# Four contiguous 256 KB transfers per token pair instead of two of 512 KB over every second row

## Chip, cores, metric

The kernel runs on one core of a Trainium2 chip. The metric is device time in microseconds (us). Before the change it took 1339.5 us (median of 3 runs, 1335.49 to 1341.65).

## The reference

```python
B, S, D, H = 64, 1024, 1024, 16          # Dh = D // H = 64
route_logits = x @ route_w               # x: [B, S, D] float32, route_w: [D, H]
best_head = np.argmax(route_logits, -1)
for h in range(H):                       # experts: [H, Dh, Dh]
    out[:, :, h, :] = (x_heads[:, :, h, :] @ experts[h]) * (best_head == h)[:, :, None]
```

x and out are 268 MB each; both have to cross between DRAM and SBUF once.

## The kernel before

The 65,536 tokens are taken 256 at a time, as a "pair" of tiles: each of the 128 partitions holds two consecutive tokens, 8 KB. A pair is loaded, transposed on TensorE, multiplied with experts and router, masked, and stored. Loads run seven pairs ahead; there are ten input and six output buffers. SP issues all of the loads and stores. An issue is the instruction that starts a transfer; the transfer has landed when all sixteen DMA engines have raised its semaphore. In the profile PE and PEld are TensorE's matmuls and weight loads, DVE is VectorE, ACT ScalarE, POOL GpSimd, SP SyncE; a q after the name is the engine's own instruction queue.

```python
WAYS = 2
XIN_BUFS, OUT_BUFS, AHEAD = 10, 6, 7     # (three lines of the kernel)
xg = x.rearrange("b s d -> (b s) d").rearrange("(g p t) d -> g p t d", p=P, t=2)
og = out.rearrange("b s d -> (b s) d").rearrange("(g p t) d -> g p t d", p=P, t=2)

def load(g):
    xin = xin_pool.tile([P, 2, D], FP32, name="xin", tag="xin")
    for r in range(WAYS):
        nc.sync.dma_start(out=xin[r::WAYS], in_=xg[g, r::WAYS])     # L106 in the profile
    return xin
# ... cut: constants, transposes (L115), split pass (L136), whole blocks (L150), ...
# ... finish(): VectorE (L173) and GpSimd (L181) write the masked products into ot
for j in range(-2 * AHEAD, NT + 2, 2):
    if j + 2 * AHEAD < NT:
        xins[j + 2 * AHEAD] = load(j // 2 + AHEAD)
    # ... cut: compute of the pair before
                if i == pair[1]:
                    for r in range(WAYS):
                        nc.sync.dma_start(out=og[i // 2, r::WAYS], in_=ot[r::WAYS])   # L223
```

The kernel names no semaphores; the framework makes them. The operands of SP's instructions in the trace show that its transfers use eight semaphores in turn, and that each issue first waits until the transfer that used its semaphore before has landed. So at most eight transfers are in flight.

## Time and profile before

| | before |
|---|---|
| time | 1339.5 us |
| TensorE busy; undisturbed pair | 96%; 4.926 us (256 x 4.926 = 1261) |
| SP's transfer queue, share of 16 engines | 98.6% |
| 8 KB data packets / 4-byte semaphore packets | 65,536 / 16,384 |
| data packet: median and floor | 309 ns |
| "held-up" time: what data packets last beyond that floor, sum of (duration - 309 ns) / 16 | 45 us per engine |
| issue to landing of a 512 KB transfer, median | 10.2 us |

The first lines are from the page of the kernel before: span, busy time of the compute engines, and the rate that the DMA engines moved in 40 equal slices of the span.

```profile
span 1338.1 us, 66342 instructions
...
PE 1290.3 (96%) x27648; PEld 1208.3 (90%) x27648; DVE 933.7 (70%) x4098; ACT 923.2 (69%) x1537; POOL 721.9 (54%) x1031
...
GB/s 340 421 421 416 413 407 409 407 407 406 412 398 377 418 417 399 395 412 414 398 393 404 410 416 418 402 408 397 410 407 410 412 407 417 416 405 416 417 409 327
```

The queue table of the kernel before gives packets, MB and the share of 16 engines' span. q1 holds SP's transfers; q8 brings instructions. The Trainium skill, "Runtime: NRT & Kernel Launch", section "Instruction fetch mechanics", says that each engine's instruction memory is refilled in blocks of 16 KiB, 256 instructions, through a DMA queue of its sequencer. This trace agrees: q8's packets have 16 KB, and TensorE's 55,296 instructions make 216 such blocks. I read q8 as TensorE's instruction fetch.

```profile
q1 hardware_dynamic: 81920, 536.94, 98.6%
q8 instruction: 218, 3.57, 1.0%
```

The chain that ended last (kernel before) is made of landings of stores, each followed by the issue that had waited for it:

```profile
DMA 96%; PE 1%; SPq 0%; DVE 0%; issue 0%; POOL 0%; ACT 0%; ACTq 0%; POOLq 0%; DVEq 0%
```

SP's own waits, kernel before (total us, times, longest): SP mostly waits for landings.

```profile
SPq L223 <- DMA out_dram<-ot: 373.2, 469, 1.7
SPq L106 <- DMA xin<-in_x_dram: 335.6, 496, 2.0
```

Issues of the kernel before, with KB each and median us from issue to landing:

```profile
xin<-in_x_dram SPq DMA_DIRECT2D x512, 512.0 KB, 10.2
out_dram<-ot SPq DMA_DIRECT2D x512, 512.0 KB, 10.2
```

SP's timeline in the middle of the kernel before (start us, length us, count). Two issues in a line of 1.7 us are each about 0.5 us long with a pause between them.

```profile
601.42 1.74 SPq L223 DMA_DIRECT2D out_dram<-ot  x2
603.92 1.68 SPq L106 DMA_DIRECT2D xin<-in_x_dram  x2
606.49 1.77 SPq L223 DMA_DIRECT2D out_dram<-ot  x2
609.03 1.65 SPq L106 DMA_DIRECT2D xin<-in_x_dram  x2
```

Waits of the compute engines, kernel before: a little time goes on output buffers whose stores are late.

```profile
DVE ot L173 <- DMA out_dram<-ot: 83.8, 104, 1.8
...
POOL ot L181 <- DMA out_dram<-ot: 76.3, 40, 3.0
```

### The profile page before, as it was taken

The page shows a single profiled execution, that of the slowest core. Times are in us where ns is not written, and L with a number is a line of the kernel's source. Part 1 is how long each engine was busy: PE and PEld are TensorE (multiplying, and loading weights), DVE is VectorE, ACT ScalarE, POOL GpSimd, SP SyncE. Part 2 cuts the span into 40 slices and gives each one's busy share as a digit, 9 for nine tenths or more (in the row PEclk, how much of TensorE's full clock was granted, in tenths as well). Part 3 has the DMA queues.
Part 4 walks back from the last instruction along what each step waited for, and adds up shares of the span by engine and source line. Part 5 has one row for each costly group of instructions (what it writes and reads, how often), then busy time and mean ns, then how long its engine had stood idle before and what let it go on. Part 6 is the DMA issues. An engine that isn't in the chain of part 4 may idle for free.

```text
span 1338.1 us, 66342 instructions
## 1 busy us (share of the span) xinstructions
PE 1290.3 (96%) x27648; PEld 1208.3 (90%) x27648; DVE 933.7 (70%) x4098; ACT 923.2 (69%) x1537; POOL 721.9 (54%) x1031
## 2 busy tenths in 40 slices
PE   7999999999999999999999999999999999999995
PEld 7888998999998999999998999889998999999995
DVE  4666766677776777777777677667777777767775
ACT  5666766767766777777676776667766767767673
POOL 3455555555555555555555555555555555555554
PEclk9999999999999999999999999999999999999998
DMA  8999999999999999999999999999999999999997
GB/s 340 421 421 416 413 407 409 407 407 406 412 398 377 418 417 399 395 412 414 398 393 404 410 416 418 402 408 397 410 407 410 412 407 417 416 405 416 417 409 327
DMA packets 84412, 541.51 MB, mean 405 GB/s; under 512 B 18576, under 2 KB 18576, under 8 KB 18576
## 3 DMA queue, kind: packets, MB, share of 16 engines
q1 hardware_dynamic: 81920, 536.94, 98.6%
q8 instruction: 218, 3.57, 1.0%
q10 hardware_dynamic: 2192, 0.33, 0.1%
q14 instruction: 82, 0.67, 0.1%
HBM read 268.76 MB, written 268.44 MB: 401 GB/s over the span
## 4 chain that ended last, share of the span: by engine, by line
DMA 96%; PE 1%; SPq 0%; DVE 0%; issue 0%; POOL 0%; ACT 0%; ACTq 0%; POOLq 0%; DVEq 0%
DMA out_dram<-ot 95%; DMA xin<-in_x_dram 1%; SPq L106 0%; PE ps_w L150 0%; PE ps_t L115 0%; DMA mv<-in_route_w_dram 0%; PE ps_s L136 0%; POOL ot L181 0%; DVE ot L173 0%; ACTq L88 0%; ACT raw L143 0%; ACT xt L117 0%; DVE mask L164 0%; POOLq L249 0%; DVE lg L158 0%
## 5 line engine op out<-in xcount | busy, mean ns | idle before, releaser
L181 POOL TENSOR_TENSOR ot<-raw,mask 128x384 f32<-128x384 f32 (+1 forms) x1024 | 721.2, 725 | 605.6 <-ACT xt L117 338.0
L117 ACT COPY xt<-ps_t 128x512 f32<-128x512 f32 x1024 | 576.7, 589 | 288.5 <-PE ps_t L115 288.0
L115 PE MATMUL ps_t<-ident,xin 128*128 128x128 f32 x4096 | 756.5, 277 | 9.7 <-DMA xin<-in_x_dram 6.9
L150 PE MATMUL ps_w<-mf,xt 128*128 128x144 f32 x3072 | 580.3, 289 | 1.5 <-DVE ot L173 1.1
L115 PEld LDWEIGHTS ps_t<-ident,xin 128*128 128x128 f32 x4096 | 499.7, 141 | 33.6 <-issue 8.9
L150 PEld LDWEIGHTS ps_w<-mf,xt 128*128 128x128 f32 x3072 | 464.2, 191 | 8.8 <-DVE ot L173 6.3
L136 PE MATMUL ps_s<-mv,xt 64*64 64x80 f32 x20480 | 430.0, 232 | 22.6 <-issue 21.9
L136 PEld LDWEIGHTS ps_s<-mv,xt 64*64 64x64 f32 x20480 | 381.1, 133 | 73.2 <-issue 62.8
L143 ACT COPY raw<-ps_s 128x704 f32<-128x704 f32 x512 | 371.1, 747 | 104.3 <-PE ps_s L136 64.9
L173 DVE TENSOR_TENSOR ot<-ps_w,mask 128x384 f32<-128x384 f32 x512 | 285.6, 558 | 98.5 <-DMA out_dram<-ot 83.8
L127 DVE TENSOR_REDUCE lgs<-ps_s 128x16 f32<-128x96 f32 x512 | 121.4, 251 | 106.3 <-ACT raw L143 105.4
L164 DVE TENSOR_SCALAR mask<-hid,ix 128x16 f32<-128x16 f32 x512 | 120.0, 234 | 56.0 <-POOL ot L181 0.9
L124 DVE TENSOR_REDUCE lgw<-ps_w 128x16 f32<-128x48 f32 x512 | 103.3, 202 | 78.9 <-PE ps_w L150 78.1
L158 DVE TENSOR_TENSOR lg<-lgs,lgw 128x16 f32<-128x16 f32 x512 | 131.8, 257 | 17.6
L160 DVE MAX8 mx<-lg 128x8 f32<-128x16 f32 x512 | 91.2, 178 | 17.6
L162 DVE FIND_INDEX8 ix<-mx,lg 128x8 uint32<-128x16 f32 x512 | 86.5, 169 | 0.0
L162 DVE MATCH_VALUE_LOAD ix<-mx,lg 128x8 f32 x512 | 47.2, 92 | 17.7
L117 ACT ACT_TABLE_LOAD x1 | 1.3, 1283 | 7.3 <-DMA mf<-in_experts_dram 7.3
L81 DVE MEMSET mf<- 128x432 f32 x1 | 0.4, 418 | 0.9 <-PEq L238 0.9
masks.py:197 POOL MEMSET ident<- 128x128 f32 x1 | 0.2, 205 | 0.3 <-POOLq L238 0.3
masks.py:199 POOL TENSOR_SCALAR_AFFINE_SELECT ident<-ident 128x128 f32<-128x128 f32 x1 | 0.3, 294 | 0.0
L238 POOL MEMSET const-float32-0.0<- 128x1 f32 x1 | 0.1, 99 | 0.2 <-issue 0.2
(5 smaller groups left out, 0.6 us busy)
## 6 DMA issues: line engine op xcount, KB each, us to landing
xin<-in_x_dram SPq DMA_DIRECT2D x512, 512.0 KB, 10.2
out_dram<-ot SPq DMA_DIRECT2D x512, 512.0 KB, 10.2
mv<-in_experts_dram ACTq DMA_DIRECT2D x2, 48.0 KB, 4.7
mf<-in_experts_dram ACTq DMA_DIRECT2D x2, 48.0 KB, 2.4
mv<-in_experts_dram ACTq DMA_DIRECT2D x2, 32.0 KB, 3.9
mv<-in_route_w_dram ACTq DMA_DIRECT2D x1, 24.0 KB, 4.6
mf<-in_route_w_dram ACTq DMA_DIRECT2D x1, 24.0 KB, 3.1
mv<-in_route_w_dram ACTq DMA_DIRECT2D x1, 16.0 KB, 3.2
```

The lines of the kernel that those rows point to most:

```text
L115: nc.tensor.transpose(ps_t[:, q, :], xin[:, t, p * P:(p + 1) * P], ident)
L117: nc.scalar.copy(out=xt[:, half * (NB // 2):(half + 1) * (NB // 2), :], in_=ps_t)
L124: nc.vector.tensor_reduce(out=lg, in_=parts.rearrange("k s h -> k h s"), op=ALU.add, axis=AX.X)
L127: nc.vector.tensor_reduce(out=lg, in_=parts.rearrange("k b s h -> k h b s"), op=ALU.add, axis=AX.XY)
L136: nc.tensor.matmul(ps[th * 64:(th + 1) * 64, half, o0:o0 + W], lhsT=xt[half * 64:(half + 1) * 64, p, th * 64:(th + 1) * 64], rhs=mv[half * ...
L143: nc.scalar.copy(out=raw[:, :, 0:RW], in_=ps[:, :, 0:RW])
L150: nc.tensor.matmul(ps[:, o0:o0 + STEP], lhsT=xt[:, NS + f, :], rhs=mf[:, f, :], start=(f == 0), stop=(f == NF - 1), skip_group_check=True)
L158: nc.vector.tensor_add(out=lg, in0=lgs, in1=lgw)
L162: nc.vector.max_index(out=ix, in_max=mx, in_values=lg)
L164: nc.vector.tensor_scalar(out=mask, in0=hid, scalar1=ix[:, 0:1], scalar2=None, op0=ALU.is_equal)
L173: nc.vector.tensor_tensor(out=ov[:, NS:], in1=bc(mk[:, NS:]), op=ALU.mult, in0=ps[:, W:W + NF * STEP].rearrange("k (f w) -> k f w", w=STEP ...
L181: nc.gpsimd.tensor_tensor(out=ov[:, ab:NS:2], in0=rv4[:, 0:n, :, o0:o0 + Dh], in1=bc(mk[:, ab:NS:2]), op=ALU.mult)
```

## The change

The intent is larger contiguous stretches of DRAM: partitions r, r+4, r+8, ... take one contiguous 256 KB of tokens. The price is four transfers per pair and direction instead of two. The mapping of tokens to partitions is the same for load and store, so the result is the same.

```diff
-WAYS = 2
+WAYS = 4
...
-    xg = x.rearrange("b s d -> (b s) d").rearrange("(g p t) d -> g p t d", p=P, t=2)
-    og = out.rearrange("b s d -> (b s) d").rearrange("(g p t) d -> g p t d", p=P, t=2)
+    xg = x.rearrange("b s d -> (b s) d").rearrange("(g r m t) d -> g r m t d", r=WAYS, t=2, m=P // WAYS)
+    og = out.rearrange("b s d -> (b s) d").rearrange("(g r m t) d -> g r m t d", r=WAYS, t=2, m=P // WAYS)
...
-            nc.sync.dma_start(out=xin[r::WAYS], in_=xg[g, r::WAYS])
+            nc.sync.dma_start(out=xin[r::WAYS], in_=xg[g, r])
...
-                        nc.sync.dma_start(out=og[i // 2, r::WAYS], in_=ot[r::WAYS])
+                        nc.sync.dma_start(out=og[i // 2, r], in_=ot[r::WAYS])
```

## The prediction

> **What bounds the kernel now.** The DMA engines. The queue table puts the SP-issued queue at 98.6% of 16 engines' span, and the chain that ended last is 95% "out_dram<-ot". The packet records show 8 KB data packets of 309 ns (median and floor; back to back they start every 306 ns) and 4-byte semaphore packets of 9 ns (every 6). Per engine: 4096 x 0.306 + 1024 x 0.006 = 1260 us. Packets held up beyond 309 ns add 45 us, instruction fetches about 13, start and tail about 20: 1338. TensorE is a close second: an undisturbed pair takes 4.926 us (spacing of the split matmuls), so 256 pairs are 1261 us plus start and end; its idle time is small and its stretched pairs (5.2 to 6.4 us) follow late output stores (DVE and POOL wait 84 and 76 us for out_dram<-ot).
>
> SP: in the SP wait table it waits 373 + 336 us for earlier DMAs. The operands show eight semaphores in rotation, so each issue waits for the landing of the transfer eight before. Landing takes 10.2 us, eight times 1.27: nearly all queueing. Unloaded, the first transfer lands in 3.9 us, of which data is 1.24.
>
> **What the change does.** Same bytes, same 8 KB packets (32 rows over 16 engines: two each instead of four). The Trainium skill, "SBUF — State Buffer", section "Door 1: The DMA port swizzle", lets partition bits 2 to 4 and 6 choose the port, so every fourth partition still reaches all 16; I expect no port gain or loss. Semaphore packets double: 1024 x 6 ns = +6 us per engine. Contiguous DRAM may shorten some of the 45 us of held-up packets; nothing in this trace says that DRAM order causes them. I credit 0 to 15 us.
>
> What it costs is issue. SP goes from 1024 to 2048 issues. Where SP did not have to wait (the first loads, the timeline from 7.4 us), issues followed every 0.64 us (595 ns plus 44); right after a wait one takes 0.47 to 0.51. ACT's issues of 128 to 384 rows took about 0.6 too, so I expect 32 rows to cost nearly as much as 64. "DMA: Bandwidth & Descriptors", section "Issuing engines are not separate DMA queues", calls issue time usually small relative to the DMA; here 0.64 us stands against 0.63 us of engine time for 256 KB. Eight issues and two semaphore instructions per pair: about 5.25 us, against 5.14 now. 256 x 5.25 + 11 of start and tail = 1355 us, if SP never waited.
>
> It also waits. Eight transfers of 256 KB in flight are 5.1 us of work; about 3.3 us of that is unloaded latency, so the backlog in front of the engines falls from some 6 us to under 2. A packet held up for 0.5 to 2.7 us on one engine then starves the other fifteen. I estimate 1 to 4% for that, partly overlapping the issue limit.
>
> **Prediction.** All of this is on the critical path: 1378 us, range 1345 to 1430. Faster by over 2%: 4%; within 2%: 31%; slower: 65%.
>
> **What would show it.** SP: 2048 issues, median still 0.47 to 0.6 us, many following after 44 ns, its wait for DMAs far below 709 us. Landing near 5 us. The queue's share of the engines below 98.6%, packets 98304, held-up time not above 45 us. TensorE waits longer, for xin or through ot; pair spacing about 5.3 us.
>
> **What would make it wrong.** Issue of 32 rows much cheaper than 64 (then near 1350); held-up packets vanishing with contiguous DRAM (towards 1320); stalls on the shallow backlog worse than estimated (over 1430).

## The result

The change takes 1583.72 us (median of 4 runs, 1579.9 to 1589.53) against 1339.34 us: a ratio of 1.183, 95% interval 1.178 to 1.188. Ratios in this document are the mean time of one kernel's fast runs over that of the other's fast runs of the same rounds, so not quite the ratio of the medians.

The same lines of the page after the change. The mean rate falls from 405 to 341 GB/s, in every slice alike; it is no matter of one phase.

```profile
span 1587.8 us, 68119 instructions
...
PE 1371.9 (86%) x27648; PEld 1219.5 (77%) x27648; DVE 971.0 (61%) x4098; ACT 919.9 (58%) x1537; POOL 720.1 (45%) x1031
...
GB/s 293 338 338 335 358 340 338 346 324 357 340 353 345 349 339 353 334 344 362 350 339 355 352 338 331 350 341 339 327 334 338 338 338 332 339 345 336 349 338 352
```

The queue table after the change: 16,384 more packets, which are the semaphore packets, and a share of 92.9%. That share is far too high for a rate 16% lower. The records explain it: data packets still have a floor of 309 ns, but held-up time has grown from 45 to 191 us per engine.

```profile
q1 hardware_dynamic: 98304, 537.00, 92.9%
q8 instruction: 219, 3.59, 0.9%
```

The chain that ended last, after the change, now has SP's own work in it with 29%:

```profile
DMA 37%; SPq 29%; PE 20%; DVE 9%; issue 4%; POOL 0%; ACTq 0%; DVEq 0%; ACT 0%; POOLq 0%
```

SP's waits after the change, as the table has them. Waits for landings are down from 709 to 40 us.

```profile
SPq L106 <- PE ps_t L115: 49.8, 90, 1.5
SPq L106 <- PE ps_w L150: 29.5, 44, 1.3
SPq L106 <- DMA xin<-in_x_dram: 27.1, 49, 2.0
SPq L223 <- DMA out_dram<-ot: 12.9, 33, 1.1
```

The two lines about PE need care. In the trace, all pauses between SP's instructions that exceed 0.12 us sum to only 58 us in the whole run. The table puts a wait down to a semaphore that happened to move near the end of a long instruction; most of those 79 us lie inside long issues.

Issues after the change, KB each and median us to landing:

```profile
xin<-in_x_dram SPq DMA_DIRECT2D x1024, 256.0 KB, 5.3
out_dram<-ot SPq DMA_DIRECT2D x1024, 256.0 KB, 5.2
```

SP's timeline after the change: issues follow each other nearly without a break, and four of them take 2.5 to 3.8 us.

```profile
599.57 1.78 SPq L223 DMA_DIRECT2D out_dram<-ot  x3
601.45 3.82 SPq L106 DMA_DIRECT2D xin<-in_x_dram  x4
605.38 2.55 SPq L223 DMA_DIRECT2D out_dram<-ot  x4
608.04 2.94 SPq L106 DMA_DIRECT2D xin<-in_x_dram  x4
```

Downstream, the compute engines wait for output buffers, and TensorE for them:

```profile
POOL ot L181 <- DMA out_dram<-ot: 469.1, 166, 5.4
DVE ot L173 <- DMA out_dram<-ot: 448.5, 236, 4.1
PEld ps_w L150 <- DVE ot L173: 268.9, 344, 2.7
```

SP's time, added up from its instructions in the two traces:

| us | before | after |
|---|---|---|
| issues | 1024 | 2048 |
| their time, first 600 ns of each | 523 | 1191 |
| their time beyond 600 ns ("stretched") | 9 | 218 |
| semaphore instructions | 18 | 14 |
| pauses up to 0.12 us | 16 | 107 |
| pauses over 0.12 us (waits) | 773 | 58 |
| sum, before the parts were rounded | 1338 | 1588 |

So after the change SP is hardly ever free. The Trainium skill, "Perfetto Trace Analysis", section "What "DMA-bound" means", lists this as one of three kinds of being DMA-bound: the issuing sequencer's track is solid DMA slices, and those slices are descriptor generation, not data movement. This trace agrees on the solid track: 1408 of 1588 us are issue slices. But a solid track need not be the only limit, and the experiments had to find that out.

A second measure, from the sixteen semaphore increments of each transfer: the first of the sixteen engines is done 4.0 us after the issue before the change and 3.1 after; the last one follows 6.2 us later before, and 2.1 us later after. Before, then, the engines work on different transfers, up to 6 us apart. (For the change this was read on the 1281 transfers of the semaphores that have no increment missing in the trace.) The mean landing time also gives how many transfers were in flight on average: 1024 x 10.30 / 1338 = 7.9 of eight before, but only 2048 x 5.24 / 1588 = 6.8 after. In the change the limit of eight was thus seldom what held SP up; SP's own pace was.

### The profile page after: what moved, and what is told of

It reads as the page before. It is cut to its first block, busy times and chain, and to the rows that moved or that the text cites. A ratio compares the mean times of both kernels' runs of the same rounds, so it can differ in the third digit from the quotient of the medians.

```text
span 1587.8 us, 68119 instructions
## 1 busy us (share of the span) xinstructions
PE 1371.9 (86%) x27648; PEld 1219.5 (77%) x27648; DVE 971.0 (61%) x4098; ACT 919.9 (58%) x1537; POOL 720.1 (45%) x1031
## 3 DMA queue, kind: packets, MB, share of 16 engines
q1 hardware_dynamic: 98304, 537.00, 92.9%
## 4 chain that ended last, share of the span: by engine, by line
DMA 37%; SPq 29%; PE 20%; DVE 9%; issue 4%; POOL 0%; ACTq 0%; DVEq 0%; ACT 0%; POOLq 0%
DMA out_dram<-ot 34%; SPq L106 14%; SPq L223 14%; PE ps_w L150 8%; PE ps_t L115 7%; PE ps_s L136 5%; DVE ot L173 5%; DMA xin<-in_x_dram 3%; DVE lg L158 1%; DVE ix L162 1%; DVE mask L164 1%; DVE mx L160 1%; POOL ot L181 0%; DVE lgw L124 0%; DVE lgs L127 0%
## 5 line engine op out<-in xcount | busy, mean ns | idle before, releaser
L150 PE MATMUL ps_w<-mf,xt 128*128 128x144 f32 x3072 | 622.1, 302 | 187.4 <-DVE ot L173 185.0
L150 PEld LDWEIGHTS ps_w<-mf,xt 128*128 128x128 f32 x3072 | 469.5, 193 | 270.7 <-DVE ot L173 268.9
L136 PE MATMUL ps_s<-mv,xt 64*64 64x80 f32 x20480 | 416.8, 232 | 5.1 <-issue 5.0
L136 PEld LDWEIGHTS ps_s<-mv,xt 64*64 64x64 f32 x20480 | 373.6, 133 | 48.6 <-DVE mask L164 36.7
L158 DVE TENSOR_TENSOR lg<-lgs,lgw 128x16 f32<-128x16 f32 x512 | 198.2, 387 | 17.6
L127 DVE TENSOR_REDUCE lgs<-ps_s 128x16 f32<-128x96 f32 x512 | 107.8, 248 | 27.1 <-ACT raw L143 27.1
```

The costliest lines, as they stand in the source:

```text
L136: nc.tensor.matmul(ps[th * 64:(th + 1) * 64, half, o0:o0 + W], lhsT=xt[half * 64:(half + 1) * 64, p, th * 64:(th + 1) * 64], rhs=mv[half * ...
L150: nc.tensor.matmul(ps[:, o0:o0 + STEP], lhsT=xt[:, NS + f, :], rhs=mf[:, f, :], start=(f == 0), stop=(f == NF - 1), skip_group_check=True)
L158: nc.vector.tensor_add(out=lg, in0=lgs, in1=lgw)
```

## The experiments

The theories: **S**, SP's issue time is the limit. **D**, the contiguous order of DRAM holds packets up. **Q**, too little data is in flight: eight transfers of 256 KB are 2 MB, where eight of 512 KB were 4 MB. **H1** and **H2** differ about held-up packets: H1, they come of an empty backlog in front of the engines; H2, each transfer brings some, whatever is in flight. Each kernel was timed beside the kernel before in three or five rounds.

| kernel | time, us | ratio to before | issues by SP | most data in flight | held up, us | stretched, us |
|---|---|---|---|---|---|---|
| before | 1339.3 | 1 | 1024 | 4 MB | 45 | 9 |
| the change | 1583.7 | 1.183 | 2048 | 2 MB | 191 | 218 |
| w4_strided | 1578.2 | 1.177 | 2048 | 2 MB | 192 | 219 |
| w2_contig | 1340.1 | 1.001 | 1024 | 4 MB | 41 | 6 |
| w2_tiny | 1651.4 | 1.234 | 2048 | 2 MB | 204 | 241 |
| w2l4s | 1395.5 | 1.041 | 1536 | 2.67 MB | 89 | 120 |
| w4l2s | 1396.1 | 1.039 | 1536 | 2.67 MB | 90 | 334 |
| w4_cols | 1610.4 | 1.200 | 2048 | 2 MB | about 180 | 114 |
| w4_act1 | 1563.1 | 1.164 | 1792 | 2 MB | 187 | 208 |
| w4_alt | 1548.5 | 1.152 | 2048 | 2 MB | 188 | 201 |
| w4_fewpe | 1551.4 | 1.155 | 2048 | 2 MB | 180 | 167 |
| w2_depth4 | 1550.4 | 1.155 | 1024 | 2 MB | 179 | 10 |
| w2_depth5 | 1359.9 | 1.013 | 1024 | 2.5 MB | 68 | 14 |
| w2_depth6 | 1346.4 | 1.004 | 1024 | 3 MB | 48 | 4 |

("Most data in flight" is eight semaphores, or the stated depth, times the mean size of a transfer: the most that is allowed, not what was there. w4_cols has packets of 2 KB, with a floor of 84 ns, and its issues are shorter, so its stretched time is not on the same footing.)

### 1. DRAM order or number of transfers: w4_strided, w2_contig

w4_strided sets WAYS to 4 in the kernel before and leaves its DRAM mapping; w2_contig sets WAYS to 2 in the change.

```diff
-WAYS = 2
+WAYS = 4        # w4_strided, from the kernel before
-WAYS = 4
+WAYS = 2        # w2_contig, from the change
```

> Four transfers of 256 KB per pair, but DRAM read and written as before (every fourth 8 KB chunk). Theory S (SP's issue time: 2048 issues of about 0.69 us, SP never waits): 1570 to 1600 us, as the change, held-up packet time about 190 us per engine. Theory D (the contiguous DRAM order holds packets up): 1340 to 1400. Theory Q (256 KB transfers leave too little in flight under eight semaphores): as S.

> Two transfers of 512 KB per pair, each a contiguous stretch of DRAM. S: 1335 to 1345, as before, since the count of issues is as before. D: well above 1400, or, if contiguous order helps, 1310 to 1325. Q: 1340.

Measured: 1578.2 us (1571.74 to 1586.33) and 1340.1 us (1334.91 to 1341.35). The order of DRAM costs nothing and gives nothing, at either size; theory D falls. The whole loss comes with the number and size of the transfers.

### 2. More issues beside large transfers: w2_tiny

```diff
             nc.sync.dma_start(out=xin[r::WAYS], in_=xg[g, r::WAYS])
+            tiny()      # and after each store: a load of 16 rows of 64 bytes into scratch
```

> The kernel before with one load of 1 KB (16 rows of 64 bytes) issued by SP after each of its transfers: 2048 issues, the large ones as before. S: 1500 to 1600, as with four transfers, although the packets of data are those of before; a tiny issue should take SP about 0.6 us too. D: 1340 to 1350. Q: also longer, as the tiny ones take half of the eight semaphores and only 2 MB of data stay in flight.

Measured: 1651.4 us, slower than the change and above the 1500 to 1600 that S had foretold, although the data still moves in 512 KB transfers. The tiny load's line in the view of its instructions (min, median and max ns of an issue) shows that it costs SP as much as a large one:

```profile
L107 SPq DMA_DIRECT2D tn<-in_route_w_dram x1024: 316/583/2267, 1.4 to 1645.9; - x171
```

The direction fits S, but as the expectation said it fits Q as well.

### 3. Between the two: w2l4s, w4l2s

```diff
-        for r in range(WAYS):            # w4l2s: four loads; w2l4s: the same edit in the stores
-            nc.sync.dma_start(out=xin[r::WAYS], in_=xg[g, r::WAYS])
+        for r in range(2 * WAYS):
+            nc.sync.dma_start(out=xin[r::2 * WAYS], in_=xg[g, r::2 * WAYS])
```

> DRAM as before; two loads of 512 KB and four stores of 256 KB per pair: 1536 issues. S: SP's work is about 1536 x 0.72 = 1110 us, below the engines' 1340, so 1340 to 1370. Q: half of the loss, 1440 to 1480. D: 1340.

> DRAM as before, four loads of 256 KB and two stores of 512 KB per pair, 1536 issues; the mirror of the run that came to 1396 us. If only the count of issues matters: 1390 to 1405. If stores are what stretches issues and holds packets up: 1345 to 1380.

Measured: 1395.5 (fast runs) and 1396.1 us. Stores are no worse than loads. w2l4s missed S's range by 26 us and Q's by 45, and in its trace SP waits 366 us, so SP was not its limit. Here S alone began to look wrong.

### 4. Relieving SP: w4_act2, w4_act1, w4_cols

w4_act2 and w4_act1 give two stores, or one, of each pair to ACT's queue, one iteration late.

```diff
-                        nc.sync.dma_start(out=og[i // 2, r], in_=ot[r::WAYS])
+                        if r < WAYS - 1:             # w4_act2: r < WAYS // 2
+                            nc.sync.dma_start(out=og[i // 2, r], in_=ot[r::WAYS])
+                        else:
+                            late.append(...)         # ACT issues it in the next iteration
```

> The change, but the third and fourth store of each pair are issued by ACT, one iteration later, after its copies of the split pass: SP has 1536 issues, ACT 512 more instructions (about 0.92 + 0.33 = 1.25 ms of work). Theory S (only SP's issue time): 1340 to 1400. H1 (packets are held up because SP issues so late that the engines' backlog is empty): held-up time falls from 190 to under 110 us per engine. H2 (each issue in itself holds packets up, whoever issues it): held-up time stays near 190 us, and the engines alone need 1480 us.

w4_act2 came to 1626.1 us and settles nothing. Its result is wrong: the late stores of the last pair are never issued. And ACT's two issues of together 1.4 us sit among its copies, so that TensorE waited 278 us for the transposed tiles that ACT was to copy.

> The change with the fourth store of each pair issued by ACT, between its copies, where it has idle time: SP has 1792 issues, ACT 256 more. S: SP's time falls by 256 x 0.73 = 185 us, to about 1400; then engines and SP together 1400 to 1450. If held-up packets alone are the limit (2048 transfers as before): 1560 to 1590. If ACT's issues delay its copies for TensorE, as when it had two stores, anything up to 1600, and ACT's waits say so.

w4_act1 gave 1563.1 us, correct. SP has 256 issues less, and in its trace it now waits for landings again:

```profile
SPq L106 <- DMA xin<-in_x_dram: 127.1, 198, 2.3
SPq L227 <- DMA out_dram<-ot: 66.9, 112, 5.8
```

S had foretold 1400 to 1450. The freed SP time turned into waits. Two other things changed with it, though. The queues share the eight semaphores, and 250 of ACT's 256 stores use the same one, so SP had in effect seven. And TensorE now waits for tiles that ACT is late to copy, lines that the change doesn't have:

```profile
PEld ps_s L136 <- ACT xt L117: 69.1, 81, 2.2
PE ps_s L136 <- ACT xt L117: 55.3, 70, 2.0
```

So this run alone doesn't refute S.

w4_cols leaves all issues with SP but gives each a cheaper shape: all 128 partitions, 2 KB of each.

```diff
-        for r in range(WAYS):
-            nc.sync.dma_start(out=xin[r::WAYS], in_=xg[g, r::WAYS])
+        for t in range(2):
+            for h in range(2):
+                c = slice(h * D // 2, (h + 1) * D // 2)
+                nc.sync.dma_start(out=xin[:, t, c], in_=xg[g, :, t, c])      # stores likewise
```

> Four transfers of 256 KB per pair and direction as in the change, 2048 issues, but each over all 128 partitions with 2 KB of each (one token, half of its columns). Transfers over 128 partitions took SP 0.34 us to issue in the run with one transfer per direction, against 0.51 for 64 rows. S (SP's issue time is the limit): SP needs some 2048 x 0.5 = 1000 us, so the engines bound again, 1340 to 1400 (2 KB packets may cost a little). If the size of 256 KB or the number of transfers is what costs, whatever the issue: 1550 or more.

Measured: 1610.4 us. SP's issues take 981 us in total instead of 1408, and SP waits for landings for much of the rest:

```profile
SPq L227 <- DMA out_dram<-ot: 252.6, 662, 1.9
SPq L108 <- DMA xin<-in_x_dram: 232.7, 577, 2.1
```

Part of this kernel's time is its own: packets of 2 KB start every 80 ns, so 16,384 per engine are 1311 us, against 1253 for the 8 KB packets. That is 58 us of the 270 that it loses. Its transfers in flight are 7.8 of eight on average, so here the landings, and no longer SP, set the pace. S as the only limit is refuted: take SP's limit away, and another stands in almost the same place.

### 5. Data in flight alone: w2_depth4, w2_depth5, w2_depth6

These are the kernel before, with its 1024 issues of 512 KB and its DRAM order, plus one dependency: a transfer is issued only when the one four (five, six) before it has landed.

```diff
+    past = []
+    def dma(dst, src):
+        d = nc.sync.dma_start(out=dst, in_=src)
+        if len(past) >= 4:                       # 5, 6
+            tc.add_manual_dep(d.ins, past[-4], ..., reason="at most 4 in flight")
+        past.append(d.ins.name)
-            nc.sync.dma_start(out=xin[r::WAYS], in_=xg[g, r::WAYS])
+            dma(xin[r::WAYS], xg[g, r::WAYS])    # stores likewise
```

> The kernel before, but each transfer is issued only when the one four before it has landed (a dependency added, none taken away): 1024 issues of 512 KB, at most 2 MB in flight, as much as eight transfers of 256 KB. Q (too little data in flight): 1450 to 1600 us, held-up time above 120 us per engine, the spread between the first and last engine's share of a transfer falls from 6.2 to about 2 us. S and H2 (issue time, number of transfers): 1335 to 1360, held-up time 45.

> The same with six in flight, 3 MB. Q: about 1396, as the two kernels with 1536 issues, which have 2 to 3 MB in flight. S and H2: 1335 to 1345.

> The kernel before with at most five transfers of 512 KB in flight, 2.5 MB. The runs with at most 2 and 3 MB came to 1550 and 1346 us; the two kernels with 1536 issues, whose eight semaphores hold 2.67 MB on average, to 1396. If the data in flight explains those too: 1400 to 1450. If their 1396 came from the number of issues: this one stays near 1350.

Measured: 1550.4 us (1542.9 to 1556.82) with four in flight, 1359.9 with five, 1346.4 with six, 1340 with eight. With 2 MB in flight the kernel loses 209 us (1550.4 - 1341.2, the kernel before of the same rounds) with no additional issue, no additional packet and an SP that waits 991 of 1555 us. Too little data in flight is by itself enough to make nearly the whole loss. The lines of w2_depth4: the waits of SP (here one line of the kernel issues loads and stores), its queue, and its landings.

```profile
SPq L106 <- DMA xin<-in_x_dram: 553.0, 507, 3.9
SPq L106 <- DMA out_dram<-ot: 391.1, 476, 2.4
```

```profile
q1 hardware_dynamic: 81920, 536.94, 93.5%
...
xin<-in_x_dram SPq DMA_DIRECT2D x512, 512.0 KB, 6.0
out_dram<-ot SPq DMA_DIRECT2D x512, 512.0 KB, 5.9
```

And w2_depth5, with one transfer more in flight:

```profile
q1 hardware_dynamic: 81920, 536.94, 98.2%
...
xin<-in_x_dram SPq DMA_DIRECT2D x512, 512.0 KB, 6.5
out_dram<-ot SPq DMA_DIRECT2D x512, 512.0 KB, 6.5
```

Bytes in flight over landing time gives the rate: with four, 4 x 524,288 B / 5.95 us = 352 GB/s; with five, 6.47 us and 405; with six, 7.71 us and 408; with eight, 10.19 us and 412. (These use median landings; the pages' mean rates over the span are 348, 396, 403 and 405.) From five up the landing time grows with the depth and the rate nearly stays: the engines are full, and a deeper queue only waits longer. At four the landing should fall to about 5.1 us to keep that rate, but it stays at 5.95: 3.7 us until the first engine is done and 2.2 until the last. Held-up time is 179 us, as in the change, without a change in the packets. So it is no cost of each transfer, and H2 falls; I read it as a symptom of engines short of work, which w2_fewpe below supports. Why the landing does not fall further is not shown.

Theory Q missed twice on the way: for w2_depth6 it had foretold about 1396, and for w2_depth5 1400 to 1450; both came out lower. The step lies between 2 and 2.5 MB, not spread over 2 to 3. So the 1396 us of w2l4s and w4l2s, which may have 2.67 MB in flight, are not explained by depth alone; in w4l2s SP was solid again (1231 us of issues, 67 us of pauses over 0.12 us), in w2l4s it was not.

### 6. What stretches the issues: w4_fewpe, w2_fewpe, w4_alt, w2_alt

Of the change's 218 us of stretched issue, 152 lie in the 367 issues that overlap an instruction fetch of q8 in time, and the long ones among them mostly end 0.2 to 0.4 us after the fetch does. (The expectation below has 124 us and 288 issues, a narrower count that a recount of the trace did not give again.) w4_fewpe makes fewer TensorE instructions.

```diff
-                for th in range(2):
-                    nc.tensor.matmul(ps[th * 64:(th + 1) * 64, half, o0:o0 + W],
-                        lhsT=xt[half * 64:(half + 1) * 64, p, th * 64:(th + 1) * 64], ...)
+                nc.tensor.matmul(ps[:, half, o0:o0 + W],
+                    lhsT=xt[half * 64:(half + 1) * 64, p, :], ...)
```

> The change, with the split pass in two matmuls of 64 x 128 weights per block instead of four of 64 x 64: 68 instead of 108 matmuls per pair, same result. TensorE's instruction fetches should fall from 219 to about 140. If a fetch stretches the issue that it meets (124 us over 288 issues), 40 to 50 us of it go: 1535 to 1545. If the meeting is a coincidence: 1580 to 1590. Should TensorE itself become slower (over 5.8 us per pair), the run tells nothing.

> The kernel before with the same lighter split pass: engines save about 5 us each of instruction fetch, SP has slack: 1330 to 1340 if the matmuls of 64 x 128 run as fast; more if they run slower, which also tells how to read the run beside it.

Fetches fell to 139, as the queue table of w4_fewpe shows:

```profile
q8 instruction: 139, 2.28, 0.6%
```

Stretched time fell by 51 us, to 167, about as expected: that in issues that overlap a fetch from 152 to 86, while that in the others rose from 66 to 81. The time fell to 1551.4 us, in neither expected range, although TensorE became slower: an undisturbed pair takes 5.773 us in this form. That is 1478 us for 256 pairs, and w2_fewpe, the same edit in the kernel before, is bound by it at 1502.1 us. Only the fall of the stretched time is to be read from w4_fewpe; how much of the 32 us is due to it can't be told beside a slower TensorE.

w2_fewpe also has 174 us of stretched issues and 167 us of held-up time, with 4 MB allowed and 1024 issues. There SP waits for compute and then issues two stores and two loads in a row; the last of the four takes 1.1 us on average. Stretching thus goes with issues in a row, not with their number alone; w2_depth4, whose issues are mostly apart, has 10 us of it at 2 MB in flight. In the same way the last store and the first loads are the long ones in the change.

w4_alt issues loads and stores in turn (stores one iteration later); w2_alt does so to the kernel before.

```diff
             nc.sync.dma_start(out=xin[r::WAYS], in_=xg[g, r])
+            if late:
+                nc.sync.dma_start(**late.pop(0))     # a store of the pair before
```

> The change with its loads and stores issued in turn (load, store, load, store) instead of four and four. In the runs so far the issues stretched most were the last store and the first two loads after stores. If the run of four stores causes that: stretched time falls from 218 to under 150 us and the time to 1500 to 1540. If order does not matter: 1575 to 1595.

> The kernel before with loads and stores issued in turn, which took 36 us off the change. There SP's issue was the limit and stretched; here SP waits for landings with time to spare: 1325 to 1345, the same, or up to 15 us less if the engines are held up less by a mixed order.

w4_alt came to 1548.5 us, but its stretched time is still 201 us, so it lies in neither range. SP is solid there too, and almost all of the 26 us between the two profiled runs are the shorter issues (1383 us instead of 1408); what shortened them is not shown. In the kernel before the same order costs 0.9% (1353.8 us, above the expected 1325 to 1345): nothing to gain.

### 7. Without TensorE: w4_copy, w2_copy

Wrong results: the transfers stay, and the compute becomes two copies.

```diff
-        # transposes, split pass, whole blocks, finish
+        nc.vector.tensor_copy(out=ot[:, 0, :], in_=xin[:, 0, :])
+        nc.scalar.copy(out=ot[:, 1, :], in_=xin[:, 1, :])
```

> Wrong results on purpose: the change's 2048 transfers and its SP issues, but TensorE, the routing and the products are gone; VectorE and ScalarE copy each pair from input to output. No TensorE instruction is fetched. If those fetches (one engine kept busy for 0.94 us every 6 us) are the disturbance that the shallow backlog can't absorb: 1330 to 1380, issues hardly stretched, held-up time under 60 us. If the disturbances lie in the transfers themselves: 1500 or more.

> The same cut of the kernel before, for comparison: engines alone, without fetches and without TensorE's pace: 1285 to 1315 in all theories.

w2_copy took 1276.0 us with 4 us of held-up time: this is what the engines can do undisturbed. w4_copy took 1473.8 us with 163 us held up and 104 us stretched. So the loss of 198 us is there without a single fetch for TensorE, and the fetches are not its cause; the expectation of 1330 to 1380 missed, and the other one, 1500 or more, by 26 us. w2_copy also tells that the kernel before pays about 65 us to compute and fetches beside its transfers.

In w4_copy the engines' share is still 98.1%, at 365 GB/s:

```profile
q1 hardware_dynamic: 98304, 537.00, 98.1%
```

### 8. Larger transfers: w1

```diff
-WAYS = 2
+WAYS = 1
```

> One transfer of 1 MB per direction and pair, 512 issues, up to 8 MB in flight. S: no issue limit, 1320 to 1345. H2: held-up time falls in proportion to the issues, to about 25 us: 1315 to 1325. H1: stays near 45 us: 1330 to 1340.

Measured: 1368.2 us (ratio 1.022, interval 1.018 to 1.027), above all that was expected; by the 2% line the verdict is unclear. Issues cost only 210 us of SP in total: one over 128 partitions takes 0.34 us for a store and 0.38 for a load (medians). But SP spends 860 us in semaphore instructions that wait before stores, by its wait table for VectorE's products, and the next load is issued only after them: on average 5.0 of the eight allowed transfers were in flight. The last slice of the span moves 222 GB/s, against 327 before. No version beat the kernel before.

## Why the prediction was wrong

- **What bounds the kernel before: right.** The engines do. Six transfers in flight are enough (1346 us), eight are not too few.
- **Ports and DRAM order: right.** w4_strided and w2_contig show no effect of the order, and data packets keep their floor of 309 ns. Packets rose to 98,304 as foreseen; the additional semaphore packets are 1024 of 9 ns per engine.
- **"about 5.25 us" per pair, "256 x 5.25 + 11 of start and tail = 1355 us, if SP never waited": the first step that failed; the issue term was mis-sized.** In the change's own trace this term fills the span. SP hardly waited (58 us), as foreseen. But the term took an issue as fixed at 0.64 us. The first 600 ns of each, the small pauses and the semaphore instructions came to 1191 + 107 + 14 = 1312 us, close to it. What the sum lacked is the 218 us by which issues stretched; I had seen 0.64 us in a stretch of loads only, on an idle machine at the start. The Trainium skill, "Perfetto Trace Analysis", section "DMA Instruction — HWDGE (DVE, Sync)", says that the profiled window of an issue runs from a wait for the lock of the descriptor generator to the release of SP, and that engines may begin before all descriptors are made because the buffer fills. That allows an issue to last longer, and no run here shows which part of the window grew.
- **"I estimate 1 to 4% for that": the second step that failed.** The estimate was that a shallower backlog would cost 13 to 54 us. In the change itself it could hardly show, since SP was later than the landings. But halving the data in flight alone (w2_depth4) costs 16%, 209 us, so with the issue term put right the sum would still have been far too low. I had subtracted an unloaded latency from 5.1 us of work and called the rest, under 2 us, a backlog that mostly suffices. Measured, the landing of the last engine did not come down to 5.1 us at 2 MB: it took 5.95 us, 3.7 until the first engine and 2.2 more until the last.
- **"held-up time not above 45": wrong, and it was the telling sign.** It rose to 191 us, and in w2_depth4 to 179 with the packets of the kernel before.
- **The two limits overlap.** At 256 KB, SP's pace, stretched as it is, gives 1584 us, and 2 MB in flight by itself 1550 (w2_depth4). Relieving SP (w4_act1, w4_cols) gives next to nothing back, with the reservations made there. The converse, 256 KB transfers with more in flight, was not tried, as the framework gives these transfers eight semaphores; so how much SP's pace alone would cost stays open. Open too are what stretches issues that follow each other, apart from the share that goes with TensorE's fetches, whether the shallow backlog has a part in that, and what separates the 1396 us of the kernels with 1536 issues from the 1360 of 2.5 MB.

## What to carry to other kernels

Where the number of transfers in flight is fixed, splitting a transfer divides the data in flight as well as multiplying the issues: check bytes in flight over landing time against the rate you need, and take the landing time of the slowest engine, not the unloaded one. A busy share near 95% of the DMA engines does not show that they are the limit; compare the rate, and look at whether packets have become longer. And when an issuing queue has turned solid, relieve it in an experiment before you call it the only limit.

## What the Trainium skill lacked or had wrong

- "Perfetto Trace Analysis", "What "DMA-bound" means", names three things that bind: engines, sequencer, SBUF reads. Data in flight is missing: the same transfers took 1550 us with 2 MB in flight, 1360 with 2.5 MB and 1346 with 3 MB.
- The same page, "DMA Engine Tracks", says that slices show busy time without idle time. If the packet records read here are those slices, time lost for want of work shows largely as longer packets: 93.5% share at 348 GB/s in w2_depth4, with a floor of 309 ns unchanged and 179 us per engine beyond it.
- "DMA: Bandwidth & Descriptors", "Issuing engines are not separate DMA queues", calls issue time usually small relative to the DMA. Against the landing, 5.2 us, it was; but at 0.69 us on average for 256 KB it exceeded the 0.61 us that the two packets on each engine take (2 x 306 ns), and it came to 1408 of 1588 us.
- No page that I found gives the issue time by shape on this chip: 0.34 to 0.38 us over 128 partitions, 0.47 to 0.51 over 64 or 32 rows after a wait, 0.59 in a row, and up to 3.2 us when stretched.
- "Runtime: NRT & Kernel Launch", "Instruction fetch mechanics", calls the cost of a block "mostly hidden". It gives no duration for a block: 218 fetches in the kernel before took a median of 0.94 us each; issues that overlapped one took 1.01 us on average in the change, the others 0.62. That the fetch is the cause of the difference is argued, not shown, and without fetches (w4_copy) the loss stayed.
